# Input projection of a two-branch decoder layer: three groups of row chunks in place of four, conditioning paced over all of them, first group begun chunk by chunk

## The chip, the cores and the metric

The kernel runs on one core of a Trainium2 chip. The metric is the device time of one execution in microseconds (us). The engines in the text: PE multiplies matrices (PEld loads its stationary operand), DVE and ACT work on vectors, POOL does a few memsets, SP issues the transfers (DMA).

## The reference, cut to what matters

One layer, 256 tokens (S), 2048 features (D):

```
mod = silu(c) @ w_ada + b_ada            # 2048 x 12288; six parts: sh1, sc1, g1, sh2, sc2, g2
h = layer_norm(x) * (1 + sc1) + sh1      # 256 x 2048
proj = h @ w_in                          # 2048 x 9760 columns: queries, keys, values, gates ...
y = merge(sparse_attention(proj), mlstm(proj)) @ w_o
x = layer_norm(ALPHA * x + g1 * y)
h = layer_norm(x) * (1 + sc2) + sh2
x = layer_norm(ALPHA * x + g2 * conv_ffn(h))
```

What matters here is the first three lines: `h` needs, for each feature, its shift `sh1` and scale `1 + sc1`, which are themselves products of silu(c) with 2048 x 4096 numbers of `w_ada`; and `proj` needs all of `h`. The change lies in the part of `proj` without the 4096 merge-gate columns, which have a stage of their own.

## The kernel before, in words

**Row chunks and conditioning.** The 2048 features are 16 chunks of 128 rows, k = 0 to 15. To condition a chunk, the kernel needs two slices of `w_ada`, one for the shift (m = 0) and one for the scale (m = 1), each 128 x 2048 numbers, 1 MB. `ada_chunk` loads a slice and multiplies it on DVE with `crow` (silu(c), the same on all partitions) with a sum along the row: one product instruction (L216) when the slice goes whole into one of the buffers adaA or adaB, two instructions of 1024 columns (L226) when it goes into the weight buffers `w`. `ring` is the list of buffers that slices take in turn; `ada_cols` ends a chunk or a pair of chunks with two additions into `modc` (L244, L245). Then `modulate_in` makes hm = nT x scale + shift on ACT (L374; nT is the normalised x, turned so that features lie on partitions), its high half hT on ACT (L376, a cast to the rounded 32-bit type) and its low half on DVE (L377).

**Weights.** A weight tile of 128 x 1024 is loaded into `w` (7 buffers) and split: high half wh on ACT (L138), low half wl on DVE (L139), four buffers each. Each product of the reference becomes three matmuls: high by high, low by high, high by low (L105). The tiles come in one sequence, numbered from 0 in `stream`. A tile of `w_in_b` holds eight pieces, each a pair of a chunk and a block of 128 columns, for 24 matmuls of 128 x 256 (ps_b, called block part below); a tile of `w_in_a` (392 columns) or `w_in_v` (512) holds two chunks (ps_a, wide part).

**Groups.** `GROUPS` cuts the 16 chunks into groups of 3, 4, 5 and 4. A group runs its blocks in the order that `order_b` gives, then the four columns of 392, then the two of 512. The results of a group are copied (first group) or added (others) into accC, accQ, accM and projA, by ACT (L709) or DVE (L711, L734). Blocks 0 to 7 (`HELD` = 4 PSUM banks) stay in PSUM over all groups. In the first group the blocks run with chunks 0 and 1 first and then with chunk 2.

**Pacing.** `tk` is a queue of generators. Each weight tile calls `work`, which adds `rate` to a credit, and each whole credit issues one step (a slice's load, with its product a call later). In group 0 the rate is 2 x 4 / 14 = 0.57, in group 1 2 x 5 / 22 = 0.45, in group 2 2 x 4 / 28 = 0.29; at a group's end `tk.drain()` runs what is left, so that a group finds all its chunks conditioned.

**What sets the order.** Outside the hand-written blocks (`manual_schedule`) a scheduler places the instructions on each engine ahead of time; every engine then runs its list in order and waits where data or a buffer is missing.

Chunk 0 and 1 are conditioned together at the start, in a hand-written block: x is loaded, normalised (xt) and turned by PE (L353), first w_ada slices run through `w` and adaA, and 12 and 4 idle matmuls (L365) fill PE ahead of it.

Of the kernel before, what the change touches and what calls it, by code (L numbers as in the profile page):

```python
# [14 lines left out]
P = 128  # L15
# [16 lines left out]
NEV = 100  # L32
GROUPS = (3, 4, 5, 4)
FIRST = 2
# [6 lines left out]
NU0, NU1 = 4, 1  # L41
NIDLE = 12, 4
OFFB, OFFA, OFFN = (16, 48), 48, 64
# [19 lines left out]
def order_b(gi):  # L63


    kn = GROUPS[gi]
    if gi == len(GROUPS) - 1:
        return [(b, range(kn)) for b in range(NBLK)]
    most = 2 * HELD + (0 if gi else 8)
    a, z = range(FIRST), range(FIRST, kn)  # L70
    first = [*range(2 * HELD, most), *range(2 * HELD)]
    return ([(b, a) for b in (range(most) if gi else first)] + [(b, z) for b in range(2 * HELD, most)]
            + [(b, z) for b in range(2 * HELD)] + [(b, range(kn)) for b in range(most, NBLK)])


@with_exitstack
def build(ctx: ExitStack, tc: tile.TileContext, d, out, dbg=None):
# [191 lines left out]
    class Ticker:  # L269
# [24 lines left out]

        def until(self, g):
            self.flush()
            while g in self.q:
                run_all(self.q.pop(0))

# [67 lines left out]
    def modulate_in(k0, k1):  # L367
        tmp = t2([P, 2, S], "hm")[:, :k1 - k0, :]
        for k in range(k0, k1):
            if k0 == 0:  # L370
                nc.vector.tensor_scalar(tmp[:, k - k0, :], nT[:, k, :], modc[:, 1, k:k + 1],
                                        modc[:, 0, k:k + 1], op0=ALU.mult, op1=ALU.add)
                continue
            nc.scalar.activation(tmp[:, k - k0, :], nT[:, k, :], AF.Identity,  # L374
                                 bias=modc[:, 0, k:k + 1], scale=modc[:, 1, k:k + 1])
        return (nc.scalar.copy(hT[:, k0:k1, 0, :], tmp),  # L376
                nc.vector.tensor_sub(hT[:, k0:k1, 1, :], tmp, hT[:, k0:k1, 0, :]))  # L377

    mods = []

    def ada_mod(k0, k1):

        while k0 < k1:
            k = min(k0 + 2, k1)
            yield from ada_cols(0, 2, k0, k, lambda k0=k0, k=k: mods.append(modulate_in(k0, k)))
# [6 lines left out]
    first = ada_mod(0, FIRST)  # L392
    idle(NIDLE[0], zr[:, :P], zr)
    with tc.manual_schedule(engines={mybir.EngineType.DVE, mybir.EngineType.Activation}):
# [32 lines left out]
        for f in todo[1:]:
            f()
        for c in range(2):
            normalise(1, c)  # L430
            for p in (2 * c, 2 * c + 1):
                turn(p, 1)
        turned(0)
        normalise(1, 2)
        turned(1)
        split0 = halves(OFFB[0])
        nc.scalar.copy(split0[0], tile0)
        normalise(1, 3)
        for p in (4, 5):
            for t in range(2):  # L440
                turn(p, t)
        for p in (2, 3):
            turned(p)
        for p in (6, 7):
            for t in range(2):
                turn(p, t)
        for f in first:
            f()
        lows.append(nc.vector.tensor_sub(split0[1], tile0, split0[0]))
        for p in (4, 5):  # L450
# [90 lines left out]

    def turn_rest():
        adaB = p0.tile([P, 2, D], F32, name="adaB", tag="t16")
        ring.extend([adaA[:, i, :] for i in range(2)] + [adaB[:, i, :] for i in range(2)])
        cyclic.append(1)

# [5 lines left out]
    def load_rest():  # L552
        nc.sync.dma_start(gb, d["ml_gate_b"][0:1, :].to_broadcast([P, 8]))
        nc.sync.dma_start(prm, d["prm"])
        msk = t2([P, P], "msk")
        nc.sync.dma_start(msk, d["msk"])
        for ins in (nc.vector.tensor_copy(maskr, msk), nc.vector.tensor_copy(selr, sel4[0:36, 0:4])):
            behind(ins, lows[-1])
# [76 lines left out]
    def stream(src, width, per, off=0):  # L635

        for i in range(src.shape[0]):
            n = tiles[0]
            tiles[0] += 1
            cut = src[i][:, :width * per]  # L640
            if n == 1:
                turn_rest()
            if n:
                t = load(cut, wide[-1] if n in (2, 3) else None)
                wh, wl = load_split(cut, off[i % 2], t, mods[n // 4] if n in (1, 4) else ())
                if n == 1:
                    for p in (6, 7):
                        turned(p)
# [15 lines left out]
    lag = []  # L664
    for gi, kn in enumerate(GROUPS):
        nxt = gi < len(GROUPS) - 1
        if nxt:
            if gi == 0:
                tk.add(ada_mod(FIRST, kn))
            tk.add(ada_mod(k0 + kn, k0 + kn + GROUPS[gi + 1]))  # L670
            rate = 2 * GROUPS[gi + 1] / (6 * kn - (4 if gi == 0 else 2))
        else:
            rate = GR1
            ring.clear()
        comp = []
# [8 lines left out]
        for b, ks in order_b(gi):  # L684
# [4 lines left out]
            whole = j < HELD  # L689
            shared = whole or (gi == 0 and j < HELD + 4)  # L690
            for k in ks:
                wh, wl = next(wb)
                o = ps[:, (b % 2) * S:(b % 2 + 1) * S]
                opening = k == 0 and (not shared or b % 2 == gi == 0)
                if tiles[0] == 1:
                    mm(o, wh, hT[:, k0 + k, 0, :], opening, False)
                    mm(o, wh, hT[:, k0 + k, 1, :], False, False)
                    lag.append((o, wl, hT[:, k0 + k, 0, :]))
# [856 lines left out]
```

## Time and profile before

| | us |
|---|---|
| median of 3 runs | 1449.16 |
| lowest, highest | 1448.26, 1449.61 |
| profiled execution | 1448.23 |
| its span | 1446.3 |
| PE busy in it | 1418.9 |
| DVE busy in it | 1061.5 |
| ACT busy in it | 700.2 |
| first matmul of the input projection begins | 25.02 |
| the merge-gate columns begin | 294.55 |

Times in the rows below are counted from the start of the span. "Busy" sums the instructions of an engine. A row of a timeline has its start, its length, engine, line, operation, output and inputs, and in brackets how long the engine had been idle and what it waited for. A row of stages has the stretch, its length, each engine's busy time with the number of instructions, the clock that PE was granted (1.00 is full), the share of the DMA engines and the rate.

### The profile page before, as it was taken

How to read it: one execution, taken by the hardware profiler on the slowest of the kernel's cores; microseconds unless marked ns; L12 is line 12 of the kernel's file. 1: busy time of each engine (PE TensorE's matmuls, PEld its weight loads, DVE VectorE, ACT ScalarE, POOL GpSimd, SP SyncE). 2: the span in 40 equal slices, each digit the busy share in tenths (PEclk: the TensorE clock that was granted, in tenths of full speed). 3: DMA queues.
4: the chain of work that ended last, by engine and by line, in shares of the span. 5: the costliest groups of instructions: out<-in, count | busy, mean ns of one | idle time of the engine just before them, and what ended most of it. 6: DMA issues, size and time to landing. Idle time of an engine off the chain costs nothing.

```text
span 1446.3 us, 23680 instructions
## 1 busy us (share of the span) xinstructions
PE 1418.9 (98%) x9361; PEld 1280.7 (89%) x9361; DVE 1061.5 (73%) x1486; ACT 700.2 (48%) x954; POOL 3.6 (0%) x10
## 2 busy tenths in 40 slices
PE   7999999999999999999999999999999999999996
PEld 6998998877777888888999999988889999998886
DVE  7889886888787898779878768755555555555566
ACT  5654344746566444445565454444334444444341
POOL 0000000000000000000000000000000000000000
PEclk8999999999999999999999999999999999999998
DMA  9999878886867999899188878866666666666661
GB/s 373 418 403 371 286 239 279 301 289 217 308 219 288 357 318 344 342 334 349 37 298 293 289 237 287 292 191 190 189 198 195 192 195 196 192 193 197 190 205 59
DMA packets 103183, 374.25 MB, mean 259 GB/s; under 512 B 11168, under 2 KB 11680, under 8 KB 102304
## 3 DMA queue, kind: packets, MB, share of 16 engines
q1 hardware_dynamic: 103072, 372.75, 75.3%
q8 instruction: 73, 1.20, 0.3%
q14 instruction: 38, 0.31, 0.1%
HBM read 370.61 MB, written 2.10 MB: 258 GB/s over the span
## 4 chain that ended last, share of the span: by engine, by line
PE 89%; DVE 6%; ACT 2%; issue 1%; DMA 1%; DVEq 0%
PE ps_up L105 33%; PE ps_d L105 17%; PE ps_mg L105 12%; PE ps_b L105 8%; PE ps_br L105 6%; PE ps_a L105 6%; PE ps_o L105 3%; DVE wl L139 2%; PE ps_s L105 1%; PE ps_y L105 1%; PE ps_hid L105 1%; DVE w L226 1%; DVE adaB L216 1%; DVE xz L1150 0%; DMA w<-in_w_o_dram 0%
## 5 line engine op out<-in xcount | busy, mean ns | idle before, releaser
L139 DVE TENSOR_TENSOR wl<-w,wh 128x1024 fp32r<-128x1024 f32 (+1 forms) x475 | 571.0, 1206 | 321.7 <-ACT wh L138 320.4
L138 ACT CAST wh<-w 128x1024 fp32r<-128x1024 f32 (+1 forms) x475 | 490.9, 1038 | 610.2 <-PE ps_up L105 184.9
L105 PE MATMUL ps_up<-h2T,wh 128*128 128x256 f32 x2816 | 480.9, 276 | 0.5 <-DVE h2T L1258 0.5
L105 PEld LDWEIGHTS ps_up<-h2T,wh 128*128 128x128 f32 x2816 | 424.4, 188 | 0.9 <-DVE h2T L1258 0.8
L105 PE MATMUL ps_up<-h2T,wl 128*128 128x256 f32 x1408 | 386.8, 276 | 0.0
L105 PEld LDWEIGHTS ps_up<-h2T,wl 128*128 128x128 f32 x1408 | 264.4, 188 | 0.0
L105 PE MATMUL ps_d<-wh,uTt 128*128 128x512 f32 (+1 forms) x704 | 205.6, 376 | 0.0
L105 PE MATMUL ps_mg<-wh,hT 128*128 128x512 f32 x512 | 169.2, 401 | 0.0
L226 DVE SCALAR_TENSOR_TENSOR w<-w,crow 128x1024 f32<-128x1024 f32 x134 | 163.0, 1219 | 3.0 <-ACT crow L197 3.0
L105 PEld LDWEIGHTS ps_d<-wh,uTt 128*128 128x128 f32 x704 | 129.2, 188 | 24.0
L105 PE MATMUL ps_b<-hT,wh 128*128 128x256 f32 x768 | 133.7, 282 | 1.5 <-ACT hT L376 1.2
L105 PE MATMUL ps_d<-wl,uTt 128*128 128x512 f32 (+1 forms) x352 | 132.2, 376 | 0.0
L105 PEld LDWEIGHTS ps_b<-hT,wh 128*128 128x128 f32 x768 | 115.6, 190 | 5.7 <-issue 3.3
L105 PEld LDWEIGHTS ps_mg<-wh,hT 128*128 128x128 f32 x512 | 96.2, 188 | 22.6 <-issue 3.1
L105 PE MATMUL ps_a<-wh,hT 128*128 128x392 f32 (+1 forms) x384 | 108.4, 359 | 0.0
L105 PE MATMUL ps_b<-hT,wl 128*128 128x256 f32 x384 | 101.2, 279 | 0.7 <-DVE wl L139 0.7
L105 PE MATMUL ps_mg<-wl,hT 128*128 128x512 f32 x256 | 100.0, 391 | 0.0
L105 PEld LDWEIGHTS ps_a<-wh,hT 128*128 128x128 f32 x384 | 70.8, 188 | 7.2 <-issue 2.1
L105 PEld LDWEIGHTS ps_d<-wl,uTt 128*128 128x128 f32 x352 | 66.1, 188 | 11.9
L105 PE MATMUL ps_a<-wl,hT 128*128 128x392 f32 (+1 forms) x192 | 69.6, 362 | 2.3 <-DVE wl L139 2.3
L105 PEld LDWEIGHTS ps_b<-hT,wl 128*128 128x128 f32 x384 | 69.7, 188 | 1.7 <-DVE wl L139 1.3
L105 PE MATMUL ps_o<-wh,mgT 128*128 128x512 f32 (+1 forms) x208 | 62.3, 381 | 0.0
(278 smaller groups left out, 1280.7 us busy)
## 6 DMA issues: line engine op xcount, KB each, us to landing
w<-in_w_up_dram SPq DMA_DIRECT2D x176, 512.0 KB, 4.3
w<-in_w_ada_dram SPq DMA_DIRECT2D x134, 512.0 KB, 4.7
w<-in_w_down_dram SPq DMA_DIRECT2D x89, 512.0 KB, 3.7
w<-in_w_mg_dram SPq DMA_DIRECT2D x64, 512.0 KB, 5.0
w<-in_w_in_b_dram SPq DMA_DIRECT2D x48, 512.0 KB, 7.0
w<-in_w_br_dram SPq DMA_DIRECT2D x32, 512.0 KB, 5.2
w<-in_w_o_dram SPq DMA_DIRECT2D x32, 512.0 KB, 5.4
adaA<-in_w_ada_dram SPq DMA_DIRECT2D x15, 1024.0 KB, 10.9
```

What stands on the lines that cost most here:

```text
L105: nc.tensor.matmul(o, lhsT, rhs, start=start, stop=stop)
L138: hi = nc.scalar.copy(wh[:, :n], t[:, :n])
L139: lows.append(nc.vector.tensor_sub(wl[:, :n], t[:, :n], wh[:, :n]))
L216: ins = nc.vector.scalar_tensor_tensor(t, t, 1.0, crow, op0=ALU.mult, op1=ALU.mult, accum_out=parts[:, row(m), k, 0:1])
L226: ins = nc.vector.scalar_tensor_tensor(t, t, 1.0, crow[:, i * 1024:(i + 1) * 1024], op0=ALU.mult, op1=ALU.mult, accum_out=parts[:, row(m), ...
```

## The change

The groups become 4, 6 and 6 chunks. All groups use the same scheme: blocks 0 to 15 run with pairs of chunks, (0, 1), (2, 3) and so on, for each pair first the 8 held blocks and then 8 more, and blocks 16 to 23 with all chunks of the group at the end. In group 0 chunks 0, 1, 2 and 3 are taken one by one. The rate becomes a constant for each group, `PACE`; nothing is drained at a group's end; instead `need(k)` forces steps of the queue, ahead of a matmul, until chunk k is conditioned. Chunks 0 to 3 are conditioned one at a time (chunks 0 and 1 in the hand-written block, high and low half of hT made by `modulate_one`, which writes the high half directly from the activation), chunks 4 to 15 in pairs. The buffers adaA and adaB are in the ring from the start, in another order. The hand-written block goes as far as the first three weight tiles and includes PE. Idle matmuls become 12 and 9. The gate bias, `prm` and the mask are loaded at tile 30 in place of tile 8.

```
-GROUPS = (3, 4, 5, 4)
+GROUPS = (4, 6, 6)
+PACE = (0.45, 0.36, 0.5)
-NIDLE = 12, 4
+NREST = 30
+NIDLE = 12, 9
...
 def order_b(gi):
-    if gi == len(GROUPS) - 1:
-        return [(b, range(kn)) for b in range(NBLK)]
-    most = 2 * HELD + (0 if gi else 8)
...
+    held, free = range(2 * HELD), range(2 * HELD, 2 * HELD + 8)
+    pairs = [(k, k + 1) for k in range(0, kn, 2)]
+    if gi:
+        parts = [(ks, g) for ks in pairs for g in (held, free)]
+    else:
+        parts = [([k], g) for ks in ((0, 1), (2,), (3,)) for g in (free, held) for k in ks]
+    return [(b, ks) for ks, g in parts for b in g] + [(b, range(kn)) for b in range(16, NBLK)]
...
+        def force(self):
             self.flush()
-            while g in self.q:
-                run_all(self.q.pop(0))
+            f = next(self.q[0], 1)
+            if f == 1:
+                self.q.pop(0)
+            elif f:
+                f()
...
+    def modulate_one(k, src):
+        tmp = t2([P, S], "hm1")
+        for o in (hT[:, k, 0, :], tmp):
+            nc.scalar.activation(o, src, AF.Identity, bias=modc[:, 0, k:k + 1], scale=modc[:, 1, k:k + 1])
+        return lambda: nc.vector.tensor_sub(hT[:, k, 1, :], tmp, hT[:, k, 0, :])
...
     adaA = pg.tile([P, 2, D], F32, name="adaA", tag="gates0")
-    ring += [None, None, adaA[:, 0, :]]
+    adas = [adaA[:, i, :] for i in range(2)]
+    ring += [None, None, *adas]
...
+    ring += [t[:, i, :] for i in range(2) for t in (adaA, adaB)]
+    cyclic.append(1)
...
+    def need(k):
+        while ready[-1] <= k:
+            tk.force()
...
-            rate = 2 * GROUPS[gi + 1] / (6 * kn - (4 if gi == 0 else 2))
+        if gi == 0:
+            tk.add(third)
+            tk.add(one_mod(3))
+            tk.add(ada_mod(kn, KD))
+        rate = PACE[gi]
...
             for k in ks:
+                need(k0 + k)
                 wh, wl = next(wb)
...
-        if nxt:
-            tk.drain()
```

**How the order moves.** In the changed kernel group 0 has tiles 0 to 23, group 1 tiles 24 to 59; tiles 24 to 27 belong to chunks 4 and 5, 28 to 31 to chunks 6 and 7, 32 to 35 to chunks 8 and 9.

DVE in the kernel before, around the start of group 1, whose tiles are 18 on (wl_768 is the low half of tile 17, wl_797 of 18, wl_827 of 19, wl_857 of 20). hT_109 is hT; the rows with adaA_111 are slice products; modc_72 the two additions; hm_789 belongs to chunks 5 and 6, which tile 20 needs first.

```order
L139 TENSOR_TENSOR wl_768<-w_765,wh_767 128x1024
L139 TENSOR_TENSOR wl_797<-w_794,wh_796 128x1024
L216 SCALAR_TENSOR_TENSOR adaA_111,parts_73<-adaA_111,crow_80 128x2048
L244 TENSOR_TENSOR modc_72<-parts_73 128x2x2
L139 TENSOR_TENSOR wl_827<-w_824,wh_826 128x1024
L245 TENSOR_TENSOR modc_72<-modc_72,head_67 128x2x2
L377 TENSOR_TENSOR hT_109<-hm_789,hT_109 128x2x256
L139 TENSOR_TENSOR wl_857<-w_854,wh_856 128x1024
```

Here the conditioning stands ahead of the low half of the tile that needs it.

DVE in the changed kernel around tile 28 (wl_1077 is its low half; wl_1107, wl_1138, wl_1175 are those of tiles 29, 30 and 31, wl_1216 of 32). hm_949 belongs to chunks 6 and 7, which tile 28 needs first.

```order
L141 TENSOR_TENSOR wl_1077<-w_1074,wh_1076 128x1024
L141 TENSOR_TENSOR wl_1107<-w_1104,wh_1106 128x1024
L141 TENSOR_TENSOR wl_1138<-w_1135,wh_1137 128x1024
L608 CAST selr_371<-prm_68 36x4
L218 SCALAR_TENSOR_TENSOR adaB_372,parts_73<-adaB_372,crow_80 128x2048
L141 TENSOR_TENSOR wl_1175<-w_1172,wh_1174 128x1024
L218 SCALAR_TENSOR_TENSOR adaB_372,parts_73<-adaB_372,crow_80 128x2048
L218 SCALAR_TENSOR_TENSOR adaA_111,parts_73<-adaA_111,crow_80 128x2048
L246 TENSOR_TENSOR modc_72<-parts_73 128x2x2
L247 TENSOR_TENSOR modc_72<-modc_72,head_67 128x2x2
L380 TENSOR_TENSOR hT_109<-hm_949,hT_109 128x2x256
L141 TENSOR_TENSOR wl_1216<-w_1213,wh_1215 128x1024
```

The conditioning of chunks 6 and 7 now stands behind the low halves of all four tiles of its own chunks, 28 to 31.

DVE in the changed kernel around tile 32 (wl_1278 is the low half of tile 34, wl_1311 of 35, wl_1345 of 36). hm_1208 belongs to chunks 8 and 9, which tile 32 needs first; maskr is a cast of the attention mask.

```order
L141 TENSOR_TENSOR wl_1278<-w_1275,wh_1277 128x1024
L218 SCALAR_TENSOR_TENSOR adaA_111,parts_73<-adaA_111,crow_80 128x2048
L141 TENSOR_TENSOR wl_1311<-w_1308,wh_1310 128x1024
L218 SCALAR_TENSOR_TENSOR adaA_111,parts_73<-adaA_111,crow_80 128x2048
L608 CAST maskr_360<-msk_1141 128x128
L246 TENSOR_TENSOR modc_72<-parts_73 128x2x2
L247 TENSOR_TENSOR modc_72<-modc_72,head_67 128x2x2
L218 SCALAR_TENSOR_TENSOR adaA_111,parts_73<-adaA_111,crow_80 128x2048
L380 TENSOR_TENSOR hT_109<-hm_1208,hT_109 128x2x256
L141 TENSOR_TENSOR wl_1345<-w_1342,wh_1344 128x1024
```

Again the conditioning stands behind the low half of the last of the four tiles that use it, and the low half of hT behind one product more.

PE in the kernel before, at the start (ps_nT are the turns of x, ps_i the idle matmuls, ps_b the first weight tiles):

```order
L365 MATMUL ps_i<-zr 128x512 x12
L353 MATMUL ps_nT<-head,xt 128x128 x8
L365 MATMUL ps_i<-zr 128x512 x4
L353 MATMUL ps_nT<-head,xt 128x128 x24
L105 MATMUL ps_b<-hT,wh 128x256 x16
L105 MATMUL ps_b<-hT,wl 128x256 x8
L105 MATMUL ps_b<-hT,wh 128x256 x4
```

PE in the changed kernel, at the same place:

```order
L372 MATMUL ps_i<-zr 128x512 x12
L358 MATMUL ps_nT<-head,xt 128x128 x8
L372 MATMUL ps_i<-zr 128x512 x9
L358 MATMUL ps_nT<-head,xt 128x128 x2
L107 MATMUL ps_b<-hT,wh 128x256 x8
L107 MATMUL ps_b<-hT,wl 128x256 x8
L107 MATMUL ps_b<-hT,wh 128x256 x8
L358 MATMUL ps_nT<-head,xt 128x128 x14
L107 MATMUL ps_b<-hT,wh 128x256 x8
L107 MATMUL ps_b<-hT,wl 128x256 x8
L107 MATMUL ps_b<-hT,wh 128x256 x8
```

Two more turns of x now suffice for the first weight tile, with chunk 0 alone; the other turns stand behind it, and the second tile, with chunk 1 alone, behind 14 of these.

More of the change, by code (lines that the diff above doesn't have):

```diff
@@ L66, in order_b @@
     kn = GROUPS[gi]
-    if gi == len(GROUPS) - 1:
-        return [(b, range(kn)) for b in range(NBLK)]
-    most = 2 * HELD + (0 if gi else 8)
[L70 to L73, printed above, removed]
+    held, free = range(2 * HELD), range(2 * HELD, 2 * HELD + 8)
[5 more added lines that the diff above has]
+    return [(b, ks) for ks, g in parts for b in g] + [(b, range(kn)) for b in range(16, NBLK)]
 @with_exitstack
@@ L356, in turned @@
     def turned(p):
+        if p == 0:
+            return nc.scalar.copy(nT[:, 1, :], psx.pop(p)[:, S:])
         return nc.scalar.copy(nT[:, 2 * p:2 * p + 2, :], psx.pop(p).rearrange("p (a b) -> p a b", a=2))
@@ L369, in modulate_in @@
         for k in range(k0, k1):
[L370 to L373, printed above, removed]
             nc.scalar.activation(tmp[:, k - k0, :], nT[:, k, :], AF.Identity,
@@ L384, in ada_mod, with one_mod, high, low @@
             k = min(k0 + 2, k1)
-            yield from ada_cols(0, 2, k0, k, lambda k0=k0, k=k: mods.append(modulate_in(k0, k)))
+            yield from ada_cols(0, 2, k0, k, lambda k0=k0, k=k: (modulate_in(k0, k), ready.append(k)))
             k0 = k
     adaA = pg.tile([P, 2, D], F32, name="adaA", tag="gates0")
-    ring += [None, None, adaA[:, 0, :]]
+    adas = [adaA[:, i, :] for i in range(2)]
+    ring += [None, None, *adas]
     zr = t2([P, 512], "zr", F32R)
     nc.gpsimd.memset(zr.bitcast(F32), 0.0)
-    first = ada_mod(0, FIRST)
+    later = []
+    def one_mod(k, low=lambda f: f()):
+        yield from ada_cols(0, 2, k, k + 1, lambda: (low(modulate_one(k, nT[:, k, :])), ready.append(k + 1)))
+    first, second, third = ada_cols(0, 2, 0, 1), one_mod(1, later.append), one_mod(2)
+    splits = [halves(OFFB[i % 2]) for i in range(3)]
+    begun = [None] * 3
+    for j in range(HELD, HELD + 4):
+        psb[j] = bank(psm, "ps_b")
+    def high(n):
+        nc.scalar.copy(splits[n][0], begun[n])
+    def low(n):
+        lows.append(nc.vector.tensor_sub(splits[n][1], begun[n], splits[n][0]))
+    def opened(n, k, b0, w, x):
+        for i in range(8):
+            b = b0 + i
+            mm(psb[b // 2][:, (b % 2) * S:(b % 2 + 1) * S], splits[n][w][:, i * P:(i + 1) * P], hT[:, k, x, :],
+               not (k or w or x or b % 2), False)
     idle(NIDLE[0], zr[:, :P], zr)
-    with tc.manual_schedule(engines={mybir.EngineType.DVE, mybir.EngineType.Activation}):
+    with tc.manual_schedule(engines={mybir.EngineType.DVE, mybir.EngineType.Activation, mybir.EngineType.PE}):
         todo = [next(first) for _ in range(2)]
@@ L400, in build @@
             f()
-        todo = [next(first) for _ in range(4)]
-        tile0 = load(d["w_in_b"][0])
+        todo = [next(first) for _ in range(2)]
+        begun[0] = load(d["w_in_b"][0])
+        sums = [next(second) for _ in range(2)]
+        for n in (1, 2):
+            begun[n] = load(d["w_in_b"][n])
         steps = []
@@ L411, in build @@
                     nmr(mvx[0])
-                    for i in range(2):
+                    for i in range(3):
                         normalise(0, i)
@@ L416, in build @@
             steps.append(g)
-        for i in range(2, 4):
-            normalise(0, i)
+        normalise(0, 3)
+        high(0)
         for p in range(4):
@@ L421, in build @@
         idle(NIDLE[1], zr[:, :P], zr)
-        for f in todo[:1]:
-            f()
+        todo[0]()
         for _ in steps[1]:
@@ L426, in build @@
         nmr(mvx[1])
[L427 to L432, printed above, removed]
-        turned(0)
+        todo[1]()
+        normalise(1, 0)
+        turn(0, 1)
+        late = modulate_one(0, psx[0][:, :S])
+        opened(0, 0, 8, 0, 0)
+        low(0)
+        late()
+        normalise(1, 1)
+        turned(0)
+        opened(0, 0, 8, 1, 0)
+        opened(0, 0, 8, 0, 1)
+        for p in range(1, 4):
+            turn(p, 1)
+        sums[0]()
+        ring += adas
+        sums.append(next(third))
         normalise(1, 2)
+        high(1)
         turned(1)
-        split0 = halves(OFFB[0])
-        nc.scalar.copy(split0[0], tile0)
         normalise(1, 3)
@@ L441, in build @@
                 turn(p, t)
-        for p in (2, 3):
-            turned(p)
+        turned(2)
+        sums[1]()
+        opened(1, 1, 8, 0, 0)
+        low(1)
+        later[0]()
+        high(2)
+        turned(3)
+        opened(1, 1, 8, 1, 0)
+        opened(1, 1, 8, 0, 1)
         for p in (6, 7):
@@ L446, in build @@
                 turn(p, t)
[L447 to L450, printed above, removed]
+        for p in range(4, 8):
             turned(p)
+            psb[p - 4] = bank(psa, "ps_b")
+        sums[2]()
+        low(2)
+        opened(2, 0, 0, 0, 0)
+        opened(2, 0, 0, 0, 1)
+        opened(2, 0, 0, 1, 0)
     ast = ExitStack()
@@ L540, in dest_b @@
         return accM[:, 2 * i - 16:2 * i - 14, :], None
[L542 to L545, printed above, removed]
+    adaB = p0.tile([P, 2, D], F32, name="adaB", tag="t16")
+    ring += [t[:, i, :] for i in range(2) for t in (adaA, adaB)]
+    cyclic.append(1)
     gsig = pa.tile([P, 2, 24], F32, name="gsig")
@@ L552, in load_rest @@
     def load_rest():
-        nc.sync.dma_start(gb, d["ml_gate_b"][0:1, :].to_broadcast([P, 8]))
-        nc.sync.dma_start(prm, d["prm"])
         msk = t2([P, P], "msk")
-        nc.sync.dma_start(msk, d["msk"])
+        for ins in (nc.sync.dma_start(gb, d["ml_gate_b"][0:1, :].to_broadcast([P, 8])),
+                    nc.sync.dma_start(prm, d["prm"]), nc.sync.dma_start(msk, d["msk"])):
+            behind(ins, wide[-1])
         for ins in (nc.vector.tensor_copy(maskr, msk), nc.vector.tensor_copy(selr, sel4[0:36, 0:4])):
@@ L640, in stream @@
             cut = src[i][:, :width * per]
[L641 to L648, printed above, removed]
-            else:
-                wh, wl = split0
-            if n == 8:
+            if n > 2:
+                t = load(cut, wide[-1] if n < 7 else None)
+                wh, wl = load_split(cut, off[i % 2], t)
+            else:
+                wh, wl = splits[n]
+            if n == NREST:
                 load_rest()
-            if n in (1, 2):
+            if n in (3, 4, 5):
                 tk.tick(1.0)
                 tk.flush()
-            elif n:
+            elif n > 5:
                 work()
@@ L689, in build @@
             whole = j < HELD
-            shared = whole or (gi == 0 and j < HELD + 4)
+            shared = j < HELD + 4
             for k in ks:
+                need(k0 + k)
                 wh, wl = next(wb)
                 o = ps[:, (b % 2) * S:(b % 2 + 1) * S]
[L694 to L698, printed above, removed]
+                opening = k == 0 and (not shared or b % 2 == 0 and (not whole or gi == 0))
+                if tiles[0] <= 3:
                     continue
-                while lag:
-                    mm(*lag.pop(0), False, False)
                 mm_b(o, wh, wl, 0, hT, k0 + k, opening, k == kn - 1 and (not shared or b % 2 == 1 and not (whole and nxt)))
@@ L712, in build @@
                 if not nxt and b == 3:
+                    ring.clear()
+                    rate = GR1
                     comp.append(compress())
@@ L720, in build @@
             for k in range(k0, k0 + kn):
+                need(k)
                 wh, wl = next(wa if c < 4 else wv)
@@ L723, in build @@
                     mm_a(pss[t][:, :aw], hT, k, t, wh, wl, k == k0, k == k0 + kn - 1)
-                if not nxt and c in (3, 4) and (k - k0) % 2:
+                if not nxt and c in (3, 4) and (k - k0) % 3 == 2:
                     next(steps)
```

11 lines of the change are left out of this document (1 added, 10 removed).

## The prediction

> **What bounds the kernel now.** I read four views in this order: the page's busy shares, busy time by stage, the chain of waits, and single instructions on the timeline.
>
> ```profile
> span 1446.3 us, 23680 instructions
> PE 1418.9 (98%) x9361; PEld 1280.7 (89%) x9361; DVE 1061.5 (73%) x1486; ACT 700.2 (48%) x954; POOL 3.6 (0%) x10
> ```
>
> PE is busy 98% of the span, and the change leaves its real matmuls as they are. So the change can win only time in which PE waits or runs at a low clock, and it loses what it adds of such time. The stages that it touches end at about 294 us:
>
> ```profile
> core 0: us, PE busy (x) PEld busy (x) DVE busy (x) ACT busy (x) POOL busy (x), PEclk, DMA share, GB/s
> 8.37:15.20 6.83, 3.32 (x18) 2.38 (x17) 6.59 (x19) 2.33 (x5) 0.00 (x0) 1.00 1.03 411
> 15.20:22.03 6.83, 5.22 (x20) 3.73 (x18) 6.72 (x13) 6.36 (x10) 0.00 (x0) 0.50 1.03 420
> 22.03:25.44 3.41, 1.56 (x10) 1.14 (x10) 2.21 (x7) 3.15 (x8) 0.00 (x0) 1.00 0.98 360
> 25.44:28.85 3.41, 3.19 (x15) 3.11 (x15) 2.61 (x3) 1.45 (x3) 0.00 (x0) 0.50 1.03 421
> 28.85:52.18 23.33, 23.32 (x203) 23.12 (x202) 20.34 (x21) 12.41 (x17) 0.00 (x0) 1.00 1.03 417
> 52.18:140.80 88.62, 85.44 (x543) 78.80 (x542) 82.92 (x99) 44.54 (x61) 0.00 (x0) 1.00 1.00 394
> 140.80:216.90 76.10, 76.10 (x542) 73.74 (x542) 64.48 (x75) 34.10 (x38) 0.00 (x0) 1.00 0.78 270
> 216.90:294.50 77.60, 77.60 (x606) 65.52 (x605) 58.52 (x96) 43.41 (x59) 1.37 (x2) 1.00 0.82 286
> ```
>
> From 8.37 to 52.18 us the transfers run at 360 to 421 GB/s with a DMA share near 1: the opening is bound by what has landed. From 52.18 to 140.8 DVE is busy 82.92 of 88.62 us. From 140.8 on PE has no gap.
>
> ```profile
> 25.75 10.12 PE ps_b L105 x74
> 35.88 16.30 PE ps_b L105 x140
> 52.18 6.27 PE ps_a L105 x35
> ...
> 76.30 1.23 DVE wl L139
> 80.36 1.24 DVE wl L139
> ...
> 140.80 41.12 PE ps_b L105 x360
> 181.92 34.98 PE ps_a L105 x180
> ```
>
> In the chain the last two rows give the price of one chunk without waits: 41.12/360 = 0.1142 us for a matmul of the block part, 34.98/180 = 0.1943 for one of the wide part, so 72 x 0.1142 + 36 x 0.1943 = 15.22 us a chunk. A weight tile of eight pieces is 24 x 0.1142 = 2.74 us.
>
> I call lost time the clock time less the useful matmul time so far. At 52.18 us 216 matmuls are done (24.67 us): 27.5 lost. At 140.8 us seven chunks are done (106.5 us): 34.3 lost. So the opening costs 27.5, the rest of the first two groups 6.8 (low halves that come late, the DVE wl rows in the chain), and group three nothing (76.1 = 5 x 15.22).
>
> **The change part by part.**
>
> *The opening.*
>
> ```profile
> 18.15 2.29 DVE L216 SCALAR_TENSOR_TENSOR adaA<-adaA,crow 128x2048 f32<-128x2048 f32 x1
> ...
> 20.37 1.22 DVE L226 SCALAR_TENSOR_TENSOR w<-w,crow 128x1024 f32<-128x1024 f32 x1
> ...
> 20.48 0.38 SPq L212 DMA_DIRECT2D adaA<-in_w_ada_dram  x1
> ...
> 22.77 0.16 DVE L244 TENSOR_TENSOR modc<-parts 128x4 f32<-128x4 f32 x1
> ...
> 25.02 0.51 PE L105 MATMUL ps_b<-hT,wh 128*128 128x256 f32 x2 [1.20 <-ACT hT L376]
> ...
> 28.92 2.29 DVE L216 SCALAR_TENSOR_TENSOR adaA<-adaA,crow 128x2048 f32<-128x2048 f32 x1 [0.78 <-DMA adaA<-in_w_ada_dram]
> ```
>
> ```profile
> prm<-in_prm_dram SPq DMA_DIRECT2D x1, 172.0 KB, 11.8
> adaA<-in_w_ada_dram SPq DMA_DIRECT2D x15, 1024.0 KB, 10.9
> ```
>
> Ahead of the first modc one chunk alone drops the product at 18.15 and two of 1024 columns from DVE (2.22 and twice about 1.2, 4.6 in all): modc at about 18.2 in place of 22.77, one activation on ACT, first matmul near 19.7 in place of 25.02. Tile 0 ends at 22.4. Chunk 1's two products then take DVE from 18.6 to 23.2 and wait for their slice; its high half is there at 26.1 and tile 1 ends at 28.9. Chunk 2's first slice can be asked for only when adaA is free again (22.9), its second at 25.1, and at 417 GB/s a slice of 1024 KB takes 2.5 us behind what is queued (the one asked for at 20.48 was used at 28.92, 8.4 later; the second here 6 later, since less is queued, so 31 to 32). Product to 34.2, chunk 2's high half at 36.6, its low half behind another product at 38.5: tiles 4 and 5 end at 43.2 (37.7, low half partly covered, and 2 x 2.74). Chunk 3 goes the same way, landed at 39, product from 39.7 (behind a low half) to 41.9, high half at 44.4, and tiles 6 and 7 end at 49.9 (44.4 + 5.5). That is 21.8 us of useful work (8 x 2.74, rounded): 28.1 lost against 27.5. So **+0.6**: the early start is spent waiting for chunks 1 to 3. Bounds: -2.5 if chunk 3 is there in time, +3 if each of chunks 2 and 3 lands 1.5 later. The nine idle matmuls (1.82 for four at 14.93, at the full clock) fill time in which PE waits; they cost 0.
>
> ```profile
> 14.93 1.82 PE L365 MATMUL ps_i<-zr 128*128 128x512 f32 x4
> ```
>
> *The rows of one conditioning and one low half before:*
>
> ```profile
> 73.72 2.28 DVE L216 SCALAR_TENSOR_TENSOR adaA<-adaA,crow 128x2048 f32<-128x2048 f32 x1
> 75.21 1.05 ACT L138 CAST wh<-w 128x1024 fp32r<-128x1024 f32 x1
> 75.92 0.08 DVE L216 DVE_READ_ACCUMULATOR adaA<-adaA,crow 128x1 f32 x1
> 76.04 0.17 DVE L244 TENSOR_TENSOR modc<-parts 128x4 f32<-128x4 f32 x1
> 76.30 1.23 DVE L139 TENSOR_TENSOR wl<-w,wh 128x1024 fp32r<-128x1024 f32 x1
> ...
> 77.44 0.16 DVE L245 TENSOR_TENSOR modc<-modc,head 128x4 f32<-128x4 f32 x1
> ...
> 77.63 1.09 ACT L374 ACTIVATE hm<-nT,modc 128x256 f32<-128x256 f32 x2 [1.37 <-DVE modc L245]
> ...
> 78.76 0.62 ACT L376 CAST hT<-hm 128x512 fp32r<-128x512 f32 x1
> ...
> 79.41 0.69 DVE L377 TENSOR_TENSOR hT<-hm,hT 128x512 fp32r<-128x512 f32 x1 [1.81 <-ACT hT L376]
> ```
>
> And the two small casts that lie on DVE between:
>
> ```profile
> 48.41 0.15 DVE L557 CAST selr<-prm 36x4 fp32r<-36x4 f32 x1
> 52.83 0.23 DVE L557 CAST maskr<-msk 128x128 fp32r<-128x128 f32 x1
> ```
>
> A low half occupies DVE for 1.14 us (76.30 to 77.44); from the start of the second modc addition to the end of the cast are 1.94 us (77.44 to 79.38). A slice product occupies DVE 2.22 us (18.15 to 20.37 above).
>
> *The waits of the second half of groups 0 and 1: -6.8.* Pacing at 0.45 a tile against 0.57 and 0.4545 before gives DVE in the last two thirds of group 0 (16 tiles) 16 low halves and 7.2 slice products, 16 x 1.14 + 7.2 x 2.22 = 34 us, beside 39 us of PE (4 x 15.22 - 8 x 2.74). I take the whole 6.8 as gone. In the four narrow columns of group 1 DVE has 12 low halves at up to 1.14 us, 12 x 0.36 = 4.3 products and eight additions, 23 us and more, beside at most 6 x 24 x 0.1943 = 28 of PE; the nearest row is the stage before, which lost 6.8 with DVE at 94%: between 0 and 3, I take +1.0, nearer to nothing since it is shorter.
>
> *The eight additions into accQ and accM and twelve into projA* that fall away on DVE stood beside a PE without gaps in the stretches after 140.8: 0. If that cover were gone, it would be DVE that gained.
>
> *Loads of gate bias, prm and msk* move from tile 8 to tile 30, on SP; prm is the largest, 172 KB or 0.4 us at the rates of the stage rows, in a stretch that has no transfer at its limit; 0. Their two casts on DVE are in the waits above.
>
> *The wait at tile 28.* What low halves and casts waited for between 52.18 and 140.8:
>
> ```profile
> L139 DVE TENSOR_TENSOR wl<-w,wh 128x1024 fp32r<-128x1024 f32 (+1 forms) x34 | 37.5, 1121 | 2.2 <-ACT wh L138 2.1
> L138 ACT CAST wh<-w 128x1024 fp32r<-128x1024 f32 (+1 forms) x34 | 32.1, 973 | 22.2 <-PE ps_b L105 13.3 <-PE ps_a L105 8.8
> ```
>
> The ACT cast waits 22.2 us for PE: a buffer of four comes free only when PE ends the tile four before, and what stands behind on DVE waits with it. In the changed order (the second piece of the order shown with the change) the conditioning of chunks 6 and 7 stands on DVE behind the low half of tile 31 and a product of a later chunk, and that low half waits for PE's end of tile 27; tile 28 needs chunk 6. So PE ends 27 and waits for work that DVE could not begin. With E26 the end of tile 26: cast of tile 30 1.05, its low half 1.14, selr 0.15, a product 2.22, low half of tile 31 1.14, two products 4.44, first modc addition 0.2, then 1.94, and some 0.35 of hand-overs (76.04 - 75.92 = 0.12 is one): E26 + 12.63, which is E27 + 9.9. The low half of hT (0.69) is covered by the 8 high matmuls (0.9). Bounds: if selr and one product are done before E26, 7.5; if a slice lands late, 12. I take **+9.9**, since each piece has its row.
>
> *The wait at tile 32.* Chunk 8 stands behind the low half of tile 35, which waits for PE's end of tile 31 (third piece). E30 + 1.15 (cast of tile 34) + 1.14 + a product 2.22 = E31 + 1.78; low half of 35 1.14, product 2.22, maskr 0.23, modc 0.2, then 1.94 and 0.25 of hand-overs: E31 + 7.75. Queued behind it is one more product ahead of the low half of hT; its slice can be asked for only at E31 + 1.8. Bounds 5.5 and 9.5, I take **+7.75**. Before has nothing of this kind: there chunks 5 and 6 are needed from tile 20 on, and their conditioning stands behind the low half of tile 19, which waits for the end of tile 15 alone (first piece): five tiles of PE work, 13.7 us, lie between.
>
> *The clock after each wait.* In the stage rows a stretch of 3.41 us in which PE was busy 1.56 is followed by one at 0.50; 8.37 to 15.20 at under half busy is followed by 6.83 at 0.50. A restart in such a stretch costs half of what is left of it, up to 1.7, and the next one may be low too: 0 to 3.4 for each wait, I take 2.3, so **+4.6**. [...]
>
> Sum: +0.6 - 6.8 + 1.0 + 9.9 + 7.75 + 4.6 = +17.05. The profiled execution took 1448.23 us (span 1446.3), so 1465.3; the median of the runs, 1449.16, lies 0.9 higher: **1466**.
>
> **Rivals.**
>
> 1. *Faster: DVE is ahead.* If the slices and products of chunks 6 and 8 are done before PE gets there, both waits and their clock go and -6.8 + 1.0 + 0.6 = -5.2 stays: 1444. It decides once the two waits together are under 5.2 us. For it: DVE has 34 us of work beside 39 in group 0. Against it: the place on DVE, behind a low half that waits for PE. 0.05.
> 2. *One wait only.* The product at tile 35 finds its data and its place early, or the forced work of the first wait brings chunks 8 and 9 along: 17.05 - 7.75 - 2.3 = +7: 1456. 0.15.
> 3. *The clock stays up*: -4.6: 1461.4. For it: a wait may fall so that it leaves both stretches half busy; against it the two rows above. 0.15.
> 4. *The opening or group 0 gains nothing*: chunks 2 and 3 late by 1.5 each, with a cold stretch (+2.4 + 3.4): 1472. 0.12.
> 5. *Nothing measurable* (a gain of 5.2 and one short wait cancel): within 0.2%, 2.9 us, about what a measurement of this kernel can tell from no change. 0.03.
>
> The forecast as it stands has 0.50. Cases 2 to 4 lie on the slower side, so slower 0.92, same 0.03, faster 0.05. The range takes in cases 2 to 4: 1454 to 1475; the forecast's own bounds (-2.5 and 0 clock below, +3, +3 and 6.8 above) give 1457 to 1473.
>
> **What would show it.** In the changed kernel's profile: a PE gap of 8 to 11 us ahead of the fifth tile of group 1 (at about 100 us: 28.7 lost, 60.9 of group 0 and 11 of four tiles), released by ACT hT, a second of 6 to 9.5 us ahead of the ninth, 11 us of work later, each followed by a stretch at 0.50; first ps_b matmul at 19 to 21 us; no gap by DVE wl between 50 and 89 us; from tile 36 on no gap. If DVE shows the product of chunk 7 before PE's end of tile 27, the step at tile 28 is wrong. If the first eight tiles end before 47 us, the opening is.

## The result and the profile after

The changed kernel takes 1467.09 us (median of 4 runs, 1466.14 to 1468.18) against 1449.32 (4 runs): ratio 1.0124, 95% interval 1.0109 to 1.0140. The forecast was 1466. The page of the changed kernel:

```profile
span 1465.0 us, 23656 instructions
PE 1420.8 (97%) x9366; PEld 1284.0 (88%) x9366; DVE 1053.5 (72%) x1465; ACT 702.1 (48%) x957; POOL 3.6 (0%) x10
```

PE is busy 2 us longer (5 more idle matmuls, and matmuls at the low clock), and the span is 18.7 us longer. The stages, cut where PE stops and starts:

```profile
core 0: us, PE busy (x) PEld busy (x) DVE busy (x) ACT busy (x) POOL busy (x), PEclk, DMA share, GB/s
20.00:23.50 3.50, 2.84 (x25) 2.75 (x24) 3.11 (x3) 2.79 (x6) 0.00 (x0) 1.00 0.83 339
23.50:27.00 3.50, 2.02 (x17) 1.54 (x15) 3.43 (x7) 3.10 (x5) 0.00 (x0) 1.00 0.54 183
...
51.10:101.70 50.60, 50.60 (x339) 48.27 (x338) 40.59 (x42) 27.46 (x39) 0.00 (x0) 1.00 1.03 417
101.70:111.67 9.97, 0.29 (x3) 0.09 (x1) 8.09 (x10) 2.75 (x4) 0.00 (x0) 0.63 1.03 418
111.67:114.60 2.93, 2.93 (x13) 2.93 (x14) 0.67 (x1) 0.00 (x0) 0.00 (x0) 0.50 1.02 421
114.60:123.91 9.31, 9.31 (x84) 9.31 (x83) 3.66 (x4) 3.15 (x3) 0.00 (x0) 1.00 0.58 217
123.91:131.78 7.87, 0.28 (x3) 0.08 (x1) 6.27 (x10) 2.75 (x4) 0.00 (x0) 0.78 0.75 278
131.78:138.40 6.62, 6.05 (x26) 5.76 (x27) 2.59 (x3) 0.00 (x0) 0.00 (x0) 0.50 0.77 295
138.40:202.60 64.20, 64.20 (x424) 61.76 (x423) 58.33 (x68) 28.40 (x33) 0.00 (x0) 1.00 0.80 281
```

From 51.1 to 101.7 us PE has no gap, where the kernel before had lost some time. Then come two holes, 101.70 to 111.67 and 123.91 to 131.78, each followed by a stretch at half clock (0.50). DVE meanwhile works (8.09 and 6.27 us): it is late, not idle. What PE waited for between 17 and 140 us (us in total, times, the longest):

```profile
PE ps_b L107 <- ACT hT L379: 17.3, 2, 9.7
PE ps_b L107 <- ACT hT L385: 2.8, 3, 1.5
PE ps_b L107 <- ACT nT L364: 1.3, 1, 1.3
PE ps_b L107 <- ACT wh L140: 0.7, 1, 0.7
PE ps_b L107 <- DVE hT L380: 0.6, 1, 0.6
```

The first row is both holes: the high half of hT for chunks 6 and 8. DVE at the first hole, in order of time, and the request of a slice on SP's queue:

```profile
88.96 2.29 DVE L218 SCALAR_TENSOR_TENSOR adaA<-adaA,crow 128x2048 f32<-128x2048 f32 x1
...
95.91 2.28 DVE L218 SCALAR_TENSOR_TENSOR adaA<-adaA,crow 128x2048 f32<-128x2048 f32 x1
98.12 0.08 DVE L218 DVE_READ_ACCUMULATOR adaA<-adaA,crow 128x1 f32 x1
98.12 3.49 DVE L141 TENSOR_TENSOR wl<-w,wh 128x1024 fp32r<-128x1024 f32 x3
101.53 0.15 DVE L608 CAST selr<-prm 36x4 fp32r<-36x4 f32 x1
101.60 2.28 DVE L218 SCALAR_TENSOR_TENSOR adaB<-adaB,crow 128x2048 f32<-128x2048 f32 x1
103.81 0.08 DVE L218 DVE_READ_ACCUMULATOR adaB<-adaB,crow 128x1 f32 x1
103.81 1.21 DVE L141 TENSOR_TENSOR wl<-w,wh 128x1024 fp32r<-128x1024 f32 x1
104.95 2.28 DVE L218 SCALAR_TENSOR_TENSOR adaB<-adaB,crow 128x2048 f32<-128x2048 f32 x1
107.16 0.07 DVE L218 DVE_READ_ACCUMULATOR adaB<-adaB,crow 128x1 f32 x1
107.16 2.28 DVE L218 SCALAR_TENSOR_TENSOR adaA<-adaA,crow 128x2048 f32<-128x2048 f32 x1
109.38 0.07 DVE L218 DVE_READ_ACCUMULATOR adaA<-adaA,crow 128x1 f32 x1
109.48 0.16 DVE L246 TENSOR_TENSOR modc<-parts 128x4 f32<-128x4 f32 x1
109.68 0.17 DVE L247 TENSOR_TENSOR modc<-modc,head 128x4 f32<-128x4 f32 x1
```

```profile
91.28 0.38 SPq L214 DMA_DIRECT2D adaA<-in_w_ada_dram  x1
```

From 98.12 on, this is the order of the second piece, instruction for instruction. By the addresses in the program the products at 95.91, 101.60 and 104.95 are of later chunks, 8 and 9; only the one at 107.16 finishes chunk 7. Its slice was asked for at 91.28, when the product at 88.96, one of chunk 6, had freed that half of adaA. The slices of chunks 8 and 9 in the other three halves had been asked for before it, at 68.98, 76.08 and 85.76. Chunk 7's slice landed 8.7 us after its request, at 100.0, so its data were there when DVE began the product at 101.60. What PE waited for in this run is therefore the place of the product on DVE, not the landing.

Lost time by stage in us (clock time less the useful matmul time begun so far, at the prediction's prices; for each kernel the profiled execution):

| | end of the opening | tile 28 reached | tile 32 reached | all waits past |
|---|---|---|---|---|
| before | 27.5 (at 52.18 us) | | | 34.0 (at 216.9) |
| changed | 29.4 (at 51.1) | 30.0 (at 101.7) | 41.2 (at 123.9) | 52.6 (at 138.4) |

The difference at the end, 18.6, is the whole change in time between these two executions, whose spans differ by 18.7 (the medians differ by 17.8): what follows costs the same.

### The profile page after: what moved, and what is told of

Its sections match the earlier page's. It is cut to its first block, busy times and chain, and to the rows that moved or that the text cites. A ratio compares the mean times of both kernels' runs of the same rounds, so it can differ in the third digit from the quotient of the medians.

```text
span 1465.0 us, 23656 instructions
## 1 busy us (share of the span) xinstructions
PE 1420.8 (97%) x9366; PEld 1284.0 (88%) x9366; DVE 1053.5 (72%) x1465; ACT 702.1 (48%) x957; POOL 3.6 (0%) x10
## 4 chain that ended last, share of the span: by engine, by line
PE 89%; DVE 1%; ACT 0%; issue 0%; DVEq 0%
PE ps_up L107 33%; PE ps_d L107 16%; PE ps_mg L107 12%; PE ps_o L107 6%; PE ps_br L107 6%; PE ps_a L107 6%; PE ps_b L107 5%; PE ps_s L107 1%; PE ps_y L107 1%; PE ps_i L372 1%; PE ps_hid L107 1%; PE ps_pT L918 0%; PE ps_n L107 0%; PE ps_n L1273 0%; PE ps_adar L261 0%; PE ps_mT L1062 0%
## 5 line engine op out<-in xcount | busy, mean ns | idle before, releaser
L107 PE MATMUL ps_b<-hT,wh 128*128 128x256 f32 x768 | 137.3, 286 | 22.7 <-ACT hT L379 17.3
L107 PEld LDWEIGHTS ps_b<-hT,wh 128*128 128x128 f32 x768 | 118.2, 194 | 28.1 <-ACT hT L379 17.7
```

The source lines that it names most:

```text
L107: nc.tensor.matmul(o, lhsT, rhs, start=start, stop=stop)
```

## The experiments

The order tells where the holes are, not why the order is so. There are three theories: (1) The ring of slice buffers. After the change, one half of adaA stands in it twice (a leftover entry and the new four), so this half takes two slices of every five, and slices of later chunks in the other halves overtake its own; the reading of chunk 7 above fits it. (2) The pace of 0.45 is too low. (3) The transfers are the limit: they run at 417 GB/s from 51 to 112 us, so the slices can't be there sooner.

**ring4.** One line:

```
-    ring += [t[:, i, :] for i in range(2) for t in (adaA, adaB)]
+    ring += [adaA[:, 0, :], adaB[:, 0, :], adaB[:, 1, :]]
```

> One line changed against the changed kernel: the ring of slice buffers has each of its four buffers once (adaA half 1, adaA half 0, adaB half 0, adaB half 1), where adaA half 1 stood twice in five. The pace stays 0.45. Theory 1 (ring): the half that stands twice takes two slices of every five, so its slices fall behind, and products of later chunks get ahead of those of chunk 7 and chunk 9; with four distinct buffers the products come in the order of the chunks, the wait at tile 28 goes (9.8 us and 1.5 of clock), the one at tile 32 falls from 7.7 to about 3 us (one cast of tile 35, then hm and hT on ACT): 1449 to 1452. Theory 2 (pace): 0.45 a tile is too low, the ring does not matter: 1465 to 1468, both waits stay. Theory 3 (transfers: 417 GB/s from 51 to 112 us are the limit): the waits shrink little, or come back as waits for weight tiles: 1458 to 1467.

Measured: 1451.53 us, ratio to before 1.0018 (1.0009 to 1.0028): 15.6 us faster than the changed kernel. No PE gap is left at tile 28, and at tile 32 one of 5.6 us (7.9 before; I had expected 3). Its stages:

```profile
51.10:101.70 50.60, 50.53 (x336) 47.60 (x335) 43.71 (x45) 30.22 (x43) 0.00 (x0) 1.00 1.03 418
113.00:118.60 5.60, 0.26 (x3) 0.06 (x2) 4.87 (x8) 2.75 (x4) 0.00 (x0) 0.72 1.03 421
```

The products now come in the order of the chunks, and DVE does 3 us more in the same first stretch (43.71 against 40.59). What I missed at tile 32 is a product of a later chunk that stands between the two modc additions:

```profile
114.22 0.15 DVE L246 TENSOR_TENSOR modc<-parts 128x4 f32<-128x4 f32 x1
114.30 2.28 DVE L218 SCALAR_TENSOR_TENSOR adaB<-adaB,crow 128x2048 f32<-128x2048 f32 x1
...
116.51 0.15 DVE L247 TENSOR_TENSOR modc<-modc,head 128x4 f32<-128x4 f32 x1
```

**pace06.** The changed kernel with `PACE = (0.6, 0.36, 0.5)`, the ring as it was.

> The changed kernel with the pace of group 0 at 0.6 a tile in place of 0.45; the ring stays at five entries. Theory 1 (ring): one product, not two, remains behind the low half of tile 31, so the wait at tile 28 is 6.5 to 7.5 us in place of 9.8; at tile 32 about 4.5 in place of 7.7; clock losses stay: 1459 to 1463. Theory 2 (pace): both waits go: 1444 to 1449. Theory 3 (transfers): no change, 1465 to 1468.

Measured: 1464.13 us, 1.0104 (1.0089 to 1.0119): 3 us gained. The gaps are 6.9 and 6.3 us. The pace alone does not do it, as theory 1 says; theory 2 falls. The time is 1 us above my interval, for two reasons: 0.6 also brings late low halves ahead of tile 28 (lost time 32.4 at 101.7 us, 30.0 in the changed kernel), and the second gap is 6.3 us, not the 4.5 that I had expected.

**ring4_pace06.** Both edits.

> Both edits: four distinct buffers in the ring and a pace of 0.6 in group 0. Theory 1: neither wait is left in the order, no clock loss: 1467.1 - 9.8 - 7.7 - 4.6 = 1445, up to 1448 if DVE, now busier in group 0, has low halves late there. Theory 3 (transfers): PE waits for slices or weight tiles instead: 1452 or more, and the DMA share stays at 1 up to tile 36.

Measured: 1448.11 us, 0.9997 (0.9987 to 1.0006). Both gaps are gone, and yet this kernel is no faster than before: the time lies at the slow end of what theory 1 allowed. Its lost time goes from 28.5 (51.1 us) to 33.5 (202.6): 5 us in small waits, as before lost 6.8. What ACT's casts of weight tiles waited for from 51 to 126 us:

```profile
L140 ACT CAST wh<-w 128x1024 fp32r<-128x1024 f32 (+1 forms) x30 | 29.1, 997 | 15.7 <-DMA w<-in_w_in_b_dram 8.7 <-PE ps_b L107 6.8
```

Now weight tiles come late: the casts wait 8.7 us for their transfer. The limit is now either DVE (92% busy from 51 to 89 us) or the transfers.

**half_slices and half_products.** Of ring4_pace06, the first leaves out half of each slice's transfer from chunk 6 on, the second half of each product:

```
+                wide.append(nc.sync.dma_start(t[:, :1024], d["w_ada"][r]))     # half_slices, k >= 6, m < 2
...
+                w = D if k < 6 or m > 1 else 1024                              # half_products
+                ins = nc.vector.scalar_tensor_tensor(t[:, :w], t[:, :w], 1.0, crow[:, :w], ...
```

> The kernel with four buffers and pace 0.6, from which half of each shift and scale slice's transfer is left out from chunk 6 on (20 slices of 512 KB in place of 1 MB); the products keep their length. Theory transfers (417 GB/s until 126 us is what keeps 5 us in groups 0 and 1): these go, 1443 to 1445. Theory DVE (busy 92% from 51 to 89 us): 1447 to 1449. The scheduler orders DVE a little otherwise, which blurs 1 us.

> The kernel with four buffers and pace 0.6, from which half of each shift and scale product on DVE is left out from chunk 6 on (1024 columns, about 1.2 us in place of 2.2); the transfers stay whole. Theory DVE: late low halves in groups 0 and 1 go, 1443 to 1445. Theory transfers: 1447 to 1449.

Measured: half_slices 1444.87 us, 0.9970 (0.9959 to 0.9982); half_products 1449.04, 1.0001 (0.9992 to 1.0010). From 51.1 to 202.6 us half_slices loses 1.6 us, half_products 5.1 and ring4_pace06 5.0. The stages 51 to 89 and 89 to 126 us, half_slices first, then half_products:

```profile
51.10:89.00 37.90, 36.89 (x231) 34.57 (x230) 35.33 (x38) 22.40 (x33) 0.00 (x0) 1.00 1.01 390
89.00:126.00 37.00, 37.00 (x313) 36.40 (x312) 34.22 (x38) 18.62 (x22) 0.00 (x0) 1.00 0.89 318
```

```profile
51.10:89.00 37.90, 35.38 (x230) 33.20 (x230) 29.42 (x36) 21.90 (x35) 0.00 (x0) 1.00 1.03 419
89.00:126.00 37.00, 37.00 (x298) 35.79 (x296) 25.22 (x33) 19.18 (x23) 0.00 (x0) 1.00 1.03 418
```

With fewer bytes DVE is as busy as ever, PE has no gap from 89 us on, and 3.4 of the 5.0 us are gone. With less DVE work the transfers stay at 419 GB/s, and as much is lost as without this edit. (The profiled execution of half_products also begins worse, 31.0 lost at 51.1 us against 28.5, so I go by what is lost after that; in half_slices the scheduler placed some instructions of DVE otherwise.) So the bytes cost time here: that is shown. That DVE costs nothing is not shown, since what half_products loses lies in other places. Of its 5.1 us, 3.8 are lost up to 101.7 us, where ring4_pace06 loses 3.1. Two of its waits (1.0 us in sum, the longer one at 69.93) follow products of chunk 5, which have their full length in all three kernels. Two more (1.5 us, at 83.63 and 84.89) follow a cast on ACT that stands behind a copy of results, and that copy waits for PE. The highest rate in any stage row read from these traces is 424 GB/s (early_k2_pace05 from 20.0 to 23.5 us, nidle4 from 16.3 to 20.0). The 418 and 419 GB/s of the rows of half_products lie 1% under it, and ring4_pace06 runs at 413 to 419 from 28 to 126 us.

**ring4_pace055.** The same with 0.55.

> Four distinct slice buffers and a pace of 0.55 in group 0, between the 0.45 that left 5.5 us of one wait and its clock at tile 32 (1451.5) and the 0.6 that left 5 us of late low halves in groups 0 and 1 (1448.1). Theory 1 (order alone): with no wait behind a low half in the order and less to do on DVE in group 0, 1445 to 1447. Theory 2 (what is saved in one place is paid in the other, since DVE and the transfers are both nearly full until the slices of chunks 8 and 9 are in): 1447.5 to 1450.

Measured: 1446.49 us (11 runs), 0.9983 (0.9974 to 0.9992). This version beats both kernels, by 2.6 us and 20.6 us. Its lost time at 202.6 us is 32.2. The time lies where the first theory of the expectation put it, but not for its reason: 3.3 us are still lost after 51 us, so the second theory holds in kind, and I had priced it too high.

**nidle4.** ring4_pace06 with `NIDLE = 12, 4`.

> The kernel with four buffers and pace 0.6, with 4 idle matmuls ahead of the first turns as before, not 9. If the 9 hold the clock up for the first weight tile: 1.5 to 3 us slower, 1449.5 to 1451. If the opening is bound by the slices of chunks 1 to 3 alone: the same, 1447.5 to 1448.5.

Measured: 1449.98 us, 1.0002 (0.9993 to 1.0011), 1.9 slower than with 9. The clock is 0.61 from 20.0 to 23.5 us, where the kernel with 9 has 1.00. So the nine idle matmuls are worth 1.9 us in the medians, but not by the clock of the first weight tile, as the expectation had it: at 36 us this kernel has lost 25.9 us and ring4_pace06 26.5. In the profile the loss comes later, where PE waits 2.9 us for chunk 2 and is granted 0.85 of the clock from 40.0 to 51.1 us (1.00 in ring4_pace06); at 51.1 us 30.8 are lost against 28.5. The profile of half_products, which has the nine, shows 0.85 in that stretch too. Why chunk 2 comes late here is left open.

**warm.** Zero-adding matmuls in the two waits of the changed kernel:

```
+                if gi == 1 and b == 0 and k in (2, 4):
+                    for _ in range(WARM[k // 2 - 1]):                 # 42, 32
+                        tc.keep_in_program_order(nc.tensor.matmul(psb[7][:64, :], identr[64:, :64],
+                            hT[64:, k0, :, :].rearrange("p a b -> p (a b)"), start=False, stop=False))
```

> The changed kernel with matmuls that add zero to a bank of the sum (identity's zero corner, 64 x 64 by 512 columns, 0.21 us each) in the two waits: 42 ahead of tile 28, 32 ahead of tile 32; the waits themselves stay. Theory (clock): of the 18 us lost 4.6 are the low clock after the waits, 1.5 and 3.2, and they go: 1462 to 1463.5. Rival (the restart is slow for another reason, or a quarter of the array does not hold the clock up): 1466 to 1468.

Measured: 1465.62 us, 1.0113 (1.0098 to 1.0128), 1.5 under the changed kernel, less than expected. The intervals of the two ratios overlap and the profiled spans differ by 0.2 us only, so the trace has to tell. The 42 matmuls take 9.87 us, 0.235 each, where I had expected 0.21. After the first wait the clock is full at once (1.00 from 111.1 to 114.0 us) and the 1.5 us of low clock are gone (lost time 39.3 both at 111.67 and at 114.6, where the changed kernel goes from 39.8 to 41.3). At the second, the eight high matmuls run at full speed (1.19 us, against 2.07 in the changed kernel) and PE then waits for the low half of hT:

```profile
129.85 1.19 PE L108 MATMUL ps_b<-hT,wh 128*128 128x256 f32 x8
134.19 0.39 PE L108 MATMUL ps_b<-hT,wh 128*128 128x256 f32 x1 [3.16 <-DVE hT L381]
```

The low half stands on DVE behind a product whose slice came late (3.28 us of waiting for its transfer), and the clock is low again after that new wait (0.59 from 134.2 to 137.7). So the price of the clock at tile 32 could not be shown alone: a transfer lay under it.

**early_k2 and early_k2_pace05.** In the kernels with the new opening the transfers fall off between 23.5 and 27 us (183 GB/s in the stage row of the changed kernel, 206 to 261 in ring4_pace06, ring4_pace055, half_products and nidle4), because the next slices wait for adaA. These two ask for chunk 2's slices earlier, in four halves through the weight buffers, with four distinct slice buffers, the first at a pace of 0.55 and the second at 0.5:

```
-        for n in (1, 2):
-            begun[n] = load(d["w_in_b"][n])
+        ring += [None, None]
+        begun[1] = load(d["w_in_b"][1])
+        extra = [next(third) for _ in range(4)]
+        begun[2] = load(d["w_in_b"][2])
...
-    ring += [t[:, i, :] for i in range(2) for t in (adaA, adaB)]
+    ring += [adaB[:, 0, :], adaB[:, 1, :]]
```

> Four buffers, pace 0.55, and the two slices of chunk 2 go through the weight buffers in four halves that are asked for right behind the first weight tiles, not through adaA after chunk 1's products. In the kernels so far the transfers fall to 183 to 260 GB/s between 23.5 and 27 us (from 417), because adaA's halves are still being read: some 2 us of transfer time left empty. If the transfers set the time up to 126 us, that hole is paid later and its filling gives 1.5 to 2.5 us: 1444 to 1445 against 1446.5. If the hole does not matter (PE waits there for chunk 1 anyway): 1446 to 1447. Slower, 1447 to 1449, if chunk 1's slices now come behind those of chunk 2.

> As the kernel with chunk 2's slices early, with a pace of 0.5 in group 0. If less conditioning in group 0 leaves weight tiles in time and the earlier start of the slices still brings chunks 8 and 9 in time: the same or up to 1 us faster, 1443 to 1445. If chunks 8 and 9 come late as at 0.45: 1447 to 1450.

Measured: 1452.60 us, 1.0023 (1.0014 to 1.0032), and 1450.02 us, 1.0006 (0.9997 to 1.0014): slower than ring4_pace055, so I was wrong. The hole in the transfers is filled, in the second kernel:

```profile
23.50:27.00 3.50, 1.84 (x15) 1.36 (x14) 3.35 (x6) 2.87 (x6) 0.00 (x0) 1.00 1.02 417
```

From 51.1 to 202.6 us the second kernel then loses only 0.8 us, the first 4.6. But at 51.1 us both have lost 33.6, not 29, because PE waits for chunk 3; in the second kernel:

```profile
49.03 2.29 PE L107 MATMUL ps_b<-hT,wh 128*128 128x256 f32 x9 [3.17 <-ACT hT L385]
```

On DVE the second modc addition of chunk 3 comes at 48.19, behind a product of chunk 4 and two low halves, an order that the scheduler chose. Putting that right by hand was not tried, and no kernel with a pace of 0.5 and the old opening was run, so whether the hole itself costs time stays open.

## Why the prediction was right, step by step

- *Opening, +0.6.* Measured: +1.9 (29.4 against 27.5), inside its bounds. The first matmul came at 20.75, not 19.7, and chunks 1 to 3 each about a microsecond later than I had it (27.2, 38.5, 45.6). The mechanism was the one forecast; the size was 1.3 short. One row was misread without harm: the idle matmuls at 14.93 did not run at the full clock, since the stage from 15.20 on has 0.50. And the 28.7 lost that the signs count up to tile 28 should be 28.1 by the sum itself; 30.0 were measured.
- *Group 0, -6.8, and group 1's narrow columns, +1.0.* Between 51.1 and 101.7 us 0.6 is lost, which is -6.2. The narrow columns cost nothing, as PE has no gap from 138.4 to 202.6. Together that is -6.2 against -5.8. But I gave the pacing as the reason and DVE as the bound. The runs say that the gain was borrowed: the low pace left slices for later, while the transfers ran at 417 GB/s. At 0.45 with four buffers (ring4) one wait of 5.6 us is left; at 0.6 (ring4_pace06) both holes are gone and 5 of the 6.8 come back. The loads of prm and the others, for which I took a stretch without a transfer at its limit, fell into that same stretch; no gap of PE followed.
- *The wait at tile 28, +9.9.* 9.96 between the two matmuls, less one matmul's 0.11: 9.85.
- *The wait at tile 32, +7.75.* 7.87 less 0.11: 7.76. The low half of hT came late too, by 0.6 us of waiting; the prediction named the place and gave it no price.
- *The clock, +4.6.* 1.45 after the first wait (lost time 39.8 to 41.3) and 3.1 after the second (49.0 to 52.6, less the 0.6 for the low half): 4.5. I had taken 2.3 for each, so the sum is right and neither part is. PE worked 2.93 us at the clock of 0.50 after the first wait (111.67 to 114.60) and 6.05 after the second (131.78 to 138.40).
- Sum of the measured: 1.9 - 6.2 + 9.85 + 7.76 + 0.6 + 4.5 = 18.4. The two spans differ by 18.7, the medians by 17.8; the forecast had 17.05. That it came so near is in part luck: the opening was 1.3 short, the narrow columns were 1.0 too dear.

So the mechanism of the two waits, an order on DVE read piece by piece, was right, and its signs came: the product of chunk 7 ran at 107.16, after PE's end of tile 27 at 101.7, and no low half held PE up between 51.1 and 101.7 us.

The rivals: "DVE is ahead" was priced at 1444. Where its condition was made true (both waits gone, ring4_pace06), the time was 1448.1. I had not put the transfers into it: with half the slices' bytes left out it was 1444.9. What the prediction did not see is why the order was so: nothing in it names the double entry in the ring. Taking that out alone was worth 15.6 us.

## What to carry to other kernels

Where a list of buffers turns in a circle, count how often each stands in it: the slices that go into a buffer that stands twice are asked for late, and work for later steps overtakes them. Read from the order what stands on a helper engine between a buffer's release and the operand that the main engine needs; with durations from the trace, that sum gave both waits here to 0.1 us. And when a stage keeps its transfers full (here a DMA share of 1.03 at 417 GB/s from 51.1 to 101.7 us), a gain in an earlier stretch that only puts transfers off can be paid later, as here at a pace of 0.6: price it by bytes before counting it.

## What the runs showed of the hardware

In the traces of the two kernels, ahead of the last microseconds, the granted clock changes at times that lie whole numbers of 3.41 us apart. Before, it falls at 15.20 and 25.44 and rises at 22.03 and 28.85; in the changed kernel it falls at 15.61, 104.36 and 128.25 and rises at 19.03, 114.60 and 138.49. Cut at such distances, the changed kernel shows around its last two rises:

```profile
111.19:114.60 3.41, 2.93 (x13) 2.93 (x14) 0.69 (x1) 0.43 (x1) 0.00 (x0) 0.50 1.02 419
...
131.66:135.08 3.42, 2.73 (x11) 2.44 (x12) 2.71 (x3) 0.07 (x1) 0.00 (x0) 0.50 0.79 296
135.08:138.49 3.41, 3.41 (x18) 3.41 (x18) 0.00 (x0) 0.00 (x0) 0.00 (x0) 0.50 0.75 296
138.49:141.90 3.41, 3.41 (x32) 3.41 (x32) 1.23 (x1) 1.44 (x2) 0.00 (x0) 1.00 0.00 0
```

The full clock followed a stretch with PE busy 86% (2.93 of 3.41) and did not follow one with 80% (2.73, broken by the wait for the low half). Up to there the two traces have ten such stretches at 0.50: the five that were followed by the full clock had PE busy 86% to 100%, the five that were followed by another low one 0% to 80%. What lets the clock fall is less plain: a stretch at 46% (before, 22.03 to 25.44) was followed by the low clock, one at 51% (changed, 8.79 to 12.20) was not, and these are too few to say more.

Matmuls of 64 x 64, a quarter of the 128 x 128 of the others, stood in the wait at tile 28 of warm, where the granted clock was 1.00 (0.63 in the same wait of the changed kernel):

```profile
101.30:111.10 9.80, 9.80 (x44) 5.43 (x43) 7.92 (x10) 2.74 (x4) 0.00 (x0) 1.00 1.03 419
```
